# A decoder trunk whose first mixer loads and sums the conditioning weights at three rates instead of one

## The chip, the cores and the metric

The kernel runs on one core of one Trainium2 chip. Its time is the device time of one execution in microseconds (us). Each kernel is run several times and the median is compared.

## What is computed

Two layers of a decoder trunk for 256 tokens of width 2048. Layer 0 mixes with an S5 state space beside a gated delta rule, layer 1 with gated linear attention; each is followed by a SwiGLU feed-forward part. Every sub-layer is conditioned by a vector c: six vectors of 2048 values per layer (shift, scale and gate of the mixer, shift, scale and gate of the feed-forward part) come from one product with a large matrix.

```python
def ada_modulation(c, w, b):                 # w: 2048 x 12288
    mod = jax.nn.silu(c) @ w + b
    return jnp.split(mod[:, None, :], 6, axis=-1)
...
for i in range(DEPTH):
    sh_m, sc_m, gt_m, sh_f, sc_f, gt_f = ada_modulation(c, aw, ab)
    h = rmsnorm(x, m_pre) * (1.0 + sc_m) + sh_m
    x = x + gt_m * rmsnorm(mixer(h), m_post)
    h = rmsnorm(x, f_pre) * (1.0 + sc_f) + sh_f
    x = x + gt_f * rmsnorm(swiglu(h, wg, wu, wd), f_post)
```

The first mixer splits `h @ w_in0` into the S5 input, the q, k and v of the delta rule, a gate z and two small columns; the outputs of both head groups go through `w_out0`.

## The kernel before, in words

**Weights.** All weights are float32 and come in tiles of 128x1024 (512 KB) through one ring of six buffers, `w`, in the order of SyncE's queue (`wraw`, L228). A weight tile of a product is split into a rounded part on ScalarE (`wh`, L159) and a remainder on VectorE (`wl`, L160), with a ring of three buffers each, and TensorE multiplies three times (`mm3`, L234 to L236). A product works through its weights in pieces of two tiles, and after each piece it calls `tick(1)`.

**Streams.** A stream is a generator with a rate. A tick adds the rate to the stream's account, and each whole unit takes one step. So the rate is steps per piece of two weight tiles. The step's instructions are written there in program order, and a scheduler then orders each engine's instructions by their data and priorities. The streams of the first mixer are `chain` (the S5 recurrence, `s5_run`), `solve` (the delta rule's matrices, then its output) and `ada` (the conditioning).

**The conditioning (`ada`).** A section of 2048 values is done in two halves of 16 weight tiles each, one tile per step. There are three sections in the first mixer's list, so 96 steps. The first, the mixer's own gate `gm0`, is in the form for TensorE: the first of each four steps loads four tiles and sums them by 16 small matmuls (`row_sums`, L329). The other two, the shift and the scale `sf0` of the feed-forward part, are in the form for VectorE: each step loads one tile and adds it, times a value of silu(c), to an accumulator of 128x1024 (L355). At the end of a half 16 small matmuls (L365) sum the accumulator over the partitions. Each half begins with a memset and two small transfers on GpSimd (L340, L341, and L398 for a gate), which stand in a fixed order in its queue.

**The first mixer (`mixer0`)**, from about 165 us to 591 us of the span, has these stages, with their ticks:

- the convolved part of `w_in0` (q, k, v): eight products of two pieces, 16 ticks, behind a small product of an eighth of a tick. After the fourth (c = 6) the stream `solve` starts. The second four are the values v.
- the gate z: two products of four pieces, 8 ticks, while `solve` does the delta rule's matrices.
- the gate of the S5 part (`s5_glu`): 4 ticks.
- the first half of `w_out0` (`out_part`): 8 ticks, beside the end of `solve` (`gdn_out`).
- the second half of `w_out0` (`post`): 8 ticks. During its last two (n = 3) `ada` is held still (`quiet`). The residual x is loaded anew here on ScalarE's queue.

After that `post` forms the root of the mean square of one token block on VectorE (L134 to L139), adds the block to x (L527), and calls `pre`, which normalises x again, turns it by matmuls (L458) and applies the shift and scale that `need("sf0")` asks for. Steps of `ada` that are still missing then are taken at once.

Of the kernel before, what the change touches and what calls it, by code (L numbers as in the profile page):

```python
# [31 lines left out]
BOOST = (100, 100, 100)  # L32

PREP = 1.4
AR = (2.2, 1.25, 1.04, 0.3)
RS = (1.2, 2.0)
RG = (1.52, 1.8, 4)

# [5 lines left out]
class Net:  # L44
# [1463 lines left out]
    def mixer0(s, h, pu, G, then):  # L1508
        nc, a = s.nc, s.a
        W = a["w_in0"]  # L1510
        K16 = list(range(16))
        cw = s.small([P, 4, 16], tag="gd_cw", bufs=1)
        cr = s.small([P, 512], tag="t", bufs=6)[:64, :P]
        s.pin(nc.scalar.dma_start(out=cr, in_=a["gdn_conv_w"].rearrange("k (m p) -> (k m) p", p=P)))
        pc = s.tp()
        nc.tensor.transpose(pc[:, :64], cr, s.ident[:64, :64])
        nc.vector.tensor_copy(cw[:].rearrange("p k m -> p (k m)"), pc[:, :64])
        nw = s.small([P, P], tag="gd_nw", bufs=1)
        s.pin(nc.scalar.dma_start(out=nw, in_=a["gdn_norm_w"].partition_broadcast(P)))
        ya, parts, ybh, ybl = [], [], [], []  # L1520
        s.stream("chain", [s.s5_run(pu, ya)], RS[0])
        s.step("chain")
        pab = s.gemm_feat(W, 4096, K16, h, nw=16)
        beta, g, gc = s.gdn_gates(pab)
        dst = []
        for c in range(0, 16, 2):
            ps = s.gemm_feat(W, 1024 + c * P, K16, h)
            if c % 4 == 0:
                dst.append(s.b(name="qkv"))
            for i in range(2):  # L1530
                o = dst[-1][:, ((c + i) % 4) * 256 : ((c + i) % 4) * 256 + 256]
                s.gdn_conv(ps[i][:, :256], c + i, o, cw)
            if c == 6:
                s.stream("solve", [s.gdn_solve(dst, beta, g, gc, parts)], RG[0])
                s.streams["chain"][1] = RS[1]
        s.streams["solve"][1] = RG[1]
        zw = []
        for n in range(2):
            ps = s.gemm_tok(W, 3072 + n * 512, 512, K16, h)
            for t in range(NT):  # L1540
                if n == 0:
                    zw.append(s.b(name="zw"))
                zs = zw[t][:, n * 512 : n * 512 + 512]
                nc.scalar.activation(out=zs, in_=ps[t], func=AF.Silu)
                zv = zs.rearrange("p (h n) -> p h n", h=4)
                nc.gpsimd.tensor_tensor(out=zv, in0=zv, in1=nw[:].unsqueeze(1).to_broadcast([P, 4, P]), op=ALU.mult)
        s.finish("chain")
        s.streams["solve"][0].append(s.gdn_out(parts, zw, ybh, ybl))
        s.streams["solve"][1] = RG[2]
        s.boost = BOOST[2]  # L1550
        yah, yal = s.s5_glu([y[0] for y in ya], [y[1] for y in ya], [y[2] for y in ya])
        y = s.out_part(a["w_out0"], list(range(8)), s.chunks(yah, yal), None)
        s.finish("solve")
        x = s.load_x(nc.scalar, late=True)
        get = s.chunks(ybh, ybl)
        s.post(a["w_out0"], list(range(8, 16)), lambda k: get(k - 8), y, x, G(), lambda t: then(x, t), 8)
        return x


    def run(s, out):  # L1560
# [13 lines left out]
        def into(S, H):  # L1574

            tiles = []

            def then(x, t):
                if not tiles:
                    tiles.extend(s.h_tiles())  # L1580
                s.pre(x[t], t, s.need(S), s.need(H), *tiles)

            return then, lambda: s.chunks(*tiles)

        def store(x, t):
            for i in range(4):
                eng = nc.scalar if i % 2 else nc.sync
                eng.dma_start(out=out[0, t * P : t * P + P, i * 512 : i * 512 + 512], in_=x[t][i // 2][:, i % 2 * 512 : i % 2 * 512 + 512])
# [4 lines left out]
        s.boost = BOOST[1]  # L1593
        s.stream("ada", ada[:s.NA], AR[0])
        then, h1 = into("sf0", "hf0")
        x = s.mixer0(h, pu, lambda: s.need("gm0"), then)
        s.boost = 1
        s.streams["ada"][1] = AR[1]
        s.streams["ada"][0] += ada[s.NA :]
        then, h2 = into("sm1", "hm1")  # L1600
        s.ffn(h1(), 0, x, lambda: s.need("gf0"), lambda t: then(x, t))
        s.streams["ada"][1] = AR[2]
        then, h3 = into("sf1", "hf1")
        s.gla(h2(), x, lambda: s.need("gm1"), lambda t: then(x, t))
        s.streams["ada"][1] = AR[3]
        s.ffn(h3(), 1, x, lambda: s.need("gf1"), lambda t: store(x, t))
# [40 lines left out]
```

## Time and profile before

| what | us |
|---|---|
| median of 3 runs | 2556.36 (2548.6 to 2563.09) |
| the profiled execution, its own time | 2552.04 |
| its span, first to last instruction | 2550.3 |
| TensorE busy in the span | 2433.1 (95%) |
| VectorE busy | 1722.2 (68%) |
| mean granted TensorE clock | 0.978 of full speed |

TensorE is busy almost everywhere, but its busy time is modelled and says little by itself. So the mixer is read by stages: how long a stage lasts, how many matmuls it holds, which engine or transfer TensorE waits for in it, and what the transfers move.

### The profile page before, as it was taken

The page shows a single profiled execution, that of the slowest core. Times are in us where ns is not written, and L with a number is a line of the kernel's source. Part 1 is how long each engine was busy: PE and PEld are TensorE (multiplying, and loading weights), DVE is VectorE, ACT ScalarE, POOL GpSimd, SP SyncE. Part 2 cuts the span into 40 slices and gives each one's busy share as a digit, 9 for nine tenths or more (in the row PEclk, how much of TensorE's full clock was granted, in tenths as well). Part 3 has the DMA queues.
Part 4 walks back from the last instruction along what each step waited for, and adds up shares of the span by engine and source line. Part 5 has one row for each costly group of instructions (what it writes and reads, how often), then busy time and mean ns, then how long its engine had stood idle before and what let it go on. Part 6 is the DMA issues. An engine that isn't in the chain of part 4 may idle for free.

```text
span 2550.3 us, 43246 instructions
## 1 busy us (share of the span) xinstructions
PE 2433.1 (95%) x17510; PEld 2141.5 (84%) x17510; DVE 1722.2 (68%) x2268; ACT 1106.1 (43%) x1385; POOL 91.1 (4%) x153
## 2 busy tenths in 40 slices
PE   5999998997999999999998999999999999999998
PEld 2578877876899899989987897787799889988996
DVE  6856786878677766777778676677655544545456
ACT  3354552435344444433435533444544444443443
POOL 1120011000000000000000000000000000000000
PEclk8999998998999999999999999999999999999999
DMA  8877566686798888998886596788467666666664
GB/s 282 322 245 261 176 214 215 204 312 226 244 313 292 305 285 290 309 317 314 289 273 216 155 289 224 242 282 271 164 215 225 197 191 194 195 190 194 195 191 140
DMA packets 299017, 615.70 MB, mean 241 GB/s; under 512 B 24368, under 2 KB 61680, under 8 KB 298816
## 3 DMA queue, kind: packets, MB, share of 16 engines
q1 hardware_dynamic: 294240, 604.32, 71.5%
q0 software_dynamic: 2304, 4.93, 0.6%
q10 hardware_dynamic: 2272, 3.68, 0.4%
q8 instruction: 137, 2.24, 0.3%
q14 instruction: 64, 0.52, 0.1%
HBM read 610.10 MB, written 2.10 MB: 240 GB/s over the span
## 4 chain that ended last, share of the span: by engine, by line
PE 77%; DVE 8%; DMA 8%; ACT 3%; issue 3%; POOL 0%; ACTq 0%; DVEq 0%; SPq 0%
PE mm L236 23%; PE mm L235 23%; PE mm L234 23%; DMA w<-in_ada_w_dram 6%; DVE wl L160 2%; DVE small L355 1%; PE tp L329 1%; PE tp L365 1%; DMA w<-in_w_out_dram 1%; ACT small L462 1%; ACT small L421 1%; PE tp L1049 1%; ACT wh L159 0%; PE tp L400 0%; DMA w<-in_w_in_dram 0%
## 5 line engine op out<-in xcount | busy, mean ns | idle before, releaser
L159 ACT CAST wh<-w 128x1024 fp32r<-128x1024 f32 x722 | 758.0, 1051 | 1095.6 <-PE mm L235 550.6
L160 DVE TENSOR_TENSOR wl<-w,wh 128x1024 fp32r<-128x1024 f32 x722 | 874.1, 1220 | 476.0 <-ACT wh L159 474.9
L236 PE MATMUL mm<-hhi,wl 128*128 128x256 f32 (+1 forms) x3104 | 865.1, 279 | 10.0 <-DVE wl L160 10.0
L234 PE MATMUL mm<-hhi,wh 128*128 128x256 f32 (+1 forms) x3104 | 866.2, 279 | 0.0
L235 PE MATMUL mm<-hlo,wh 128*128 128x256 f32 (+1 forms) x3104 | 863.3, 278 | 0.0
L236 PEld LDWEIGHTS mm<-hhi,wl 128*128 128x128 f32 (+1 forms) x3104 | 582.8, 188 | 15.2 <-DVE wl L160 13.2
L235 PEld LDWEIGHTS mm<-hlo,wh 128*128 128x128 f32 (+1 forms) x3104 | 583.2, 188 | 2.0 <-issue 1.1
L234 PEld LDWEIGHTS mm<-hhi,wh 128*128 128x128 f32 (+1 forms) x3104 | 581.3, 187 | 4.1 <-issue 2.0
L355 DVE SCALAR_TENSOR_TENSOR small<-w,silu_c,small 128x1024 f32<-128x1024 f32 x288 | 369.0, 1281 | 195.8 <-DMA w<-in_ada_w_dram 187.3
L236 PE MATMUL mm<-wh,alo 128*128 128x512 f32 x656 | 258.2, 394 | 0.0
L235 PE MATMUL mm<-wl,ahi 128*128 128x512 f32 x656 | 256.9, 392 | 0.0
L234 PE MATMUL mm<-wh,ahi 128*128 128x512 f32 x656 | 256.2, 391 | 0.0
L234 PE MATMUL mm<-wh,hhi 128*128 128x512 f32 x440 | 177.1, 406 | 8.1 <-DVE hhi L467 4.2
L235 PE MATMUL mm<-wl,hhi 128*128 128x512 f32 x440 | 177.8, 404 | 3.5 <-DVE wl L160 2.2
L236 PE MATMUL mm<-wh,hlo 128*128 128x512 f32 x440 | 175.2, 399 | 0.7 <-DVE hlo L468 0.7
L235 PEld LDWEIGHTS mm<-wl,ahi 128*128 128x128 f32 x656 | 123.1, 188 | 29.1 <-issue 0.5
L234 PEld LDWEIGHTS mm<-wh,ahi 128*128 128x128 f32 x656 | 123.2, 188 | 27.2 <-ACT wh L159 0.5
L236 PEld LDWEIGHTS mm<-wh,alo 128*128 128x128 f32 x656 | 123.3, 188 | 25.1
L234 PEld LDWEIGHTS mm<-wh,hhi 128*128 128x128 f32 x440 | 83.8, 192 | 27.7 <-ACT wh L159 5.5
L236 PEld LDWEIGHTS mm<-wh,hlo 128*128 128x128 f32 x440 | 84.6, 192 | 22.3 <-issue 2.3
L235 PEld LDWEIGHTS mm<-wl,hhi 128*128 128x128 f32 x440 | 84.4, 192 | 22.4 <-DVE wl L160 3.9
L329 PE MATMUL tp<-w,silu_c 128*32 128x512 f32 x384 | 67.0, 645 | 11.6 <-DMA w<-in_ada_w_dram 6.7
(438 smaller groups left out, 2325.5 us busy)
## 6 DMA issues: line engine op xcount, KB each, us to landing
w<-in_ada_w_dram SPq DMA_DIRECT2D x384, 512.0 KB, 5.2
w<-in_ffn_gate_dram SPq DMA_DIRECT2D x176, 512.0 KB, 4.6
w<-in_ffn_up_dram SPq DMA_DIRECT2D x176, 512.0 KB, 4.5
w<-in_ffn_down_dram SPq DMA_DIRECT2D x176, 512.0 KB, 4.5
w<-in_w_in_dram SPq DMA_DIRECT2D x160, 512.0 KB, 5.2
w<-in_w_out_dram SPq DMA_DIRECT2D x64, 512.0 KB, 5.3
w<-in_s_glu_w_dram SPq DMA_DIRECT2D x8, 512.0 KB, 5.0
x<-in_x_dram SPq DMA_DIRECT2D x4, 512.0 KB, 6.4
```

The costliest lines, as they stand in the source:

```text
L159: s.nc.scalar.copy(hi, x)
L160: s.subs.append(s.nc.vector.tensor_tensor(out=lo, in0=x, in1=hi, op=ALU.subtract).ins)
L234: mm(ps, lhsT=lhs[0], rhs=rhs[0], start=st, stop=False)
L235: mm(ps, lhsT=lhs[0], rhs=rhs[1], start=False, stop=False)
L236: mm(ps, lhsT=lhs[1], rhs=rhs[0], start=False, stop=en)
L329: s.nc.tensor.matmul(ps[32 * j : 32 * j + 32, :], lhsT=lhsT, rhs=w, start=first, stop=last)
L355: nc.vector.scalar_tensor_tensor(out=acc, in0=wv[:, 0], scalar=s.sc[:, g : g + 1], in1=acc, op0=ALU.mult, op1=ALU.add)
L365: s.nc.tensor.matmul(ps[:, m : m + 1], lhsT=acc[:, m * P : m * P + P], rhs=e[:, 0:1], start=True, stop=True)
L421: s.nc.scalar.activation(out=dump[:, : int(x.free_size())], in_=x, func=AF.Square, accum_out=out)
L462: nc.scalar.activation(out=hf[:, js], in_=ps[:, js], func=AF.Identity, scale=S[:, k : k + 1], bias=H[:, k : k + 1])
L1049: nc.tensor.matmul(pp[:, i * 64 : i * 64 + 64], lhsT=s.s5_win[ig][e][:, i * P : i * P + P], rhs=us[:, i * 64 : i * 64 + 64], start=True, s ...
```

## The change

The rate of `ada` in the first mixer was 2.2 throughout. It is now 3.2 up to c = 6 (8 of the 16 ticks of q, k and v), 1.6 during the values, and 2.6 from the gate z on.

```diff
-AR = (2.2, 1.25, 1.04, 0.3)
+AR = (3.2, 1.25, 1.04, 0.3)
+AM = (1.6, 2.6)
...
             if c == 6:
                 s.stream("solve", [s.gdn_solve(dst, beta, g, gc, parts)], RG[0])
                 s.streams["chain"][1] = RS[1]
+                s.streams["ada"][1] = AM[0]
         s.streams["solve"][1] = RG[1]
+        s.streams["ada"][1] = AM[1]
```

The 96 steps and all other work are the same; only places change. In the code after the change the line numbers are higher by two (L230 is L228, L529 is L527). Three places follow.

SyncE's queue at the start of the mixer: `w<-in_ada_w_dram 128x1024` is a conditioning tile, `w<-in_w_in_dram` a tile of the mixer's own weights. Before:

```order
L228 DMA w<-in_w_in_dram 128x16x16
L228 DMA w<-in_w_in_dram 128x4x256 x2
L228 DMA w<-in_ada_w_dram 128x1024 x4
L228 DMA w<-in_w_in_dram 128x4x256 x4
L228 DMA w<-in_ada_w_dram 128x1024 x4
```

After:

```order
L230 DMA w<-in_w_in_dram 128x16x16
L230 DMA w<-in_w_in_dram 128x4x256 x2
L230 DMA w<-in_ada_w_dram 128x1024 x4
L230 DMA w<-in_w_in_dram 128x4x256 x2
L230 DMA w<-in_ada_w_dram 128x1024 x4
```

The second group of four conditioning tiles now stands two weight tiles earlier; so do later ones, until seven of the eight groups are in the first half of q, k and v.

SyncE's queue at the end of the mixer, before:

```order
L228 DMA w<-in_w_out_dram 128x2x512 x2
L228 DMA w<-in_ada_w_dram 128x1024 x2
L228 DMA w<-in_w_out_dram 128x2x512 x4
L228 DMA w<-in_ada_w_dram 128x1024 x4
L228 DMA w<-in_ffn_gate_dram 128x2x512 x8
```

After:

```order
L230 DMA w<-in_w_out_dram 128x2x512 x2
L230 DMA w<-in_ada_w_dram 128x1024 x3
L230 DMA w<-in_w_out_dram 128x2x512 x12
L230 DMA w<-in_ffn_gate_dram 128x2x512 x8
L230 DMA w<-in_ffn_up_dram 128x2x512 x2
```

The last twelve tiles of `w_out0` stand alone, and the four conditioning tiles behind them are gone.

VectorE at the end of the mixer, where the first token block's root (L134 to L139) leads to the addition to x (L527). L514 takes a finished product out of PSUM, L374 finishes a piece of the scale `sf0`. Before:

```order
L134 TENSOR_SCALAR small<-small 128x1
L355 SCALAR_TENSOR_TENSOR small<-w,silu_c,small 128x1024
L136 TENSOR_SCALAR small<-small 128x1
L514 TENSOR_TENSOR y<-mm,y 128x512
L138 TENSOR_SCALAR small<-small 128x1
L355 SCALAR_TENSOR_TENSOR small<-w,silu_c,small 128x1024
L139 SCALAR_TENSOR_TENSOR small<-small 128x1
L160 TENSOR_TENSOR wl<-w,wh 128x1024
L138 TENSOR_SCALAR small<-small 128x1
L374 SCALAR_TENSOR_TENSOR S_sf_102<-tp,vcols 128x4
```

After:

```order
L516 TENSOR_TENSOR y<-mm,y 128x512
L518 TENSOR_TENSOR y<-y,gate 128x512
L136 TENSOR_SCALAR small<-small 128x1
L138 TENSOR_SCALAR small<-small 128x1
L140 TENSOR_SCALAR small<-small 128x1
L141 SCALAR_TENSOR_TENSOR small<-small 128x1
L140 TENSOR_SCALAR small<-small 128x1
L141 SCALAR_TENSOR_TENSOR small<-small 128x1
```

The root's small instructions now stand next to each other; the conditioning's sums (L355 before), its L374 and two remainders (L160) between them have gone elsewhere.

## Rows read from the trace of the kernel before

**Rows 1.** The page, part 1: busy us, share of the span, instructions.
```profile
PE 2433.1 (95%) x17510; PEld 2141.5 (84%) x17510; DVE 1722.2 (68%) x2268; ACT 1106.1 (43%) x1385; POOL 91.1 (4%) x153
```

**Rows 2.** Windows by stage: length, busy us of engines, clock, DMA share, GB/s.
```profile
165.00:246.00 81.00, 76.89 (x688) 63.09 (x686) 47.56 (x76) 37.14 (x54) 8.64 (x17) 0.98 0.71 231
246.00:332.00 86.00, 81.14 (x800) 72.60 (x799) 66.05 (x117) 44.86 (x65) 3.62 (x9) 0.98 0.62 208
332.00:428.00 96.00, 83.42 (x1334) 70.26 (x1334) 75.03 (x100) 38.32 (x52) 16.51 (x21) 0.89 0.62 205
428.00:472.00 44.00, 44.00 (x619) 42.58 (x615) 30.65 (x41) 24.05 (x41) 0.00 (x0) 0.89 0.63 206
472.00:536.00 64.00, 56.83 (x274) 46.30 (x274) 55.32 (x111) 26.38 (x35) 1.50 (x2) 0.95 0.73 244
536.00:591.50 55.50, 50.00 (x210) 38.84 (x208) 43.30 (x51) 21.22 (x32) 1.43 (x2) 0.94 0.90 324
591.50:616.50 25.00, 12.60 (x61) 11.69 (x60) 19.83 (x52) 12.81 (x35) 1.99 (x3) 0.66 0.40 130
```

**Rows 3.** PE timeline, two neighbouring matmuls of the mixer's last product: start, us.
```profile
576.00 0.39 PE L235 MATMUL mm<-wl,ybhi 128*128 128x512 f32 x1
576.23 0.39 PE L236 MATMUL mm<-wh,yblo 128*128 128x512 f32 x1
```

**Rows 4.** What PE waited for in 536:591.5: us, times, longest.
```profile
PE mm L234 <- ACT wh L159: 3.9, 2, 3.5
```

**Rows 5.** DVE timeline at the mixer's end: start, us.
```profile
588.58 0.68 DVE L514 TENSOR_TENSOR y<-mm,y 128x512 f32<-128x512 f32 x1
...
590.98 0.20 DVE L134 TENSOR_SCALAR small<-small 128x1 f32<-128x1 f32 x1
591.10 1.27 DVE L355 SCALAR_TENSOR_TENSOR small<-w,silu_c,small 128x1024 f32<-128x1024 f32 x1
...
599.65 2.74 DVE L527 SCALAR_TENSOR_TENSOR x<-y,small,x 128x512 f32<-128x512 f32 x4
```

**Rows 6.** PE timeline at the mixer's end; in brackets the idle time before.
```profile
594.46 3.57 PE L365 MATMUL tp<-ones,small 128*128 128x1 f32 x16 [2.96 <-DVE small L355]
606.38 3.97 PE L458 MATMUL tp<-small,x 128*128 128x128 f32 x17 [8.35 <-issue]
```

**Rows 7.** DVE timeline at the end of the first feed-forward part.
```profile
1369.95 0.69 DVE L514 TENSOR_TENSOR y<-mm,y 128x512 f32<-128x512 f32 x1 [0.93 <-PE mm L236]
...
1374.04 2.08 DVE L527 SCALAR_TENSOR_TENSOR x<-y,small,x 128x512 f32<-128x512 f32 x3
```

**Rows 8.** Windows of line L329 alone (row sums): length, PE and PEld busy.
```profile
165.00:246.00 81.00, 12.84 (x80) 2.49 (x80) 0.98 0.71 231
246.00:332.00 86.00, 5.77 (x48) 1.25 (x48) 0.98 0.62 208
```

**Rows 9.** Windows of line L355 alone: length, DVE busy.
```profile
246.00:332.00 86.00, 3.83 (x3) 0.98 0.62 208
332.00:428.00 96.00, 25.55 (x20) 0.89 0.62 205
428.00:472.00 44.00, 11.53 (x9) 0.89 0.63 206
472.00:536.00 64.00, 20.49 (x16) 0.95 0.73 244
536.00:591.50 55.50, 18.30 (x15) 0.94 0.90 324
```

**Rows 10.** SyncE's queue, timeline: start, us, transfers issued.
```profile
198.50 2.84 SPq L228 DMA_DIRECT2D w<-in_ada_w_dram  x4
201.45 8.38 SPq L228 DMA_DIRECT2D w<-in_w_in_dram  x4
209.92 4.84 SPq L228 DMA_DIRECT2D w<-in_ada_w_dram  x4
```

**Rows 11.** The chain of waits, 140:640, at the third group.
```profile
200.99 7.30 DMA w<-in_ada_w_dram
208.34 1.92 PE tp L329 x8
```

**Rows 12.** What PE waited for in 472:536.
```profile
PE tp L537 <- DVE small L1428: 5.1, 3, 3.7
```

## The prediction
> **What bounds the kernel now.** I read four views: the page's busy times, the windows by stage, the waits of TensorE by stage, and VectorE's timeline at the mixer's end. The page says only that TensorE has little room [rows 1]; the change acts in the first mixer alone, so the stages decide [rows 2].
>
> The last product (536 to 591.5) is not bound by its matmuls. They follow each other at 0.23 us [rows 3], so its 8 ticks of 24 need 8 x 24 x 0.228 = 43.8 us; it lasts 55.5. Its transfers run at 0.90 busy and 324 GB/s [rows 2], and TensorE waits 3.9 us for a weight's rounded part [rows 4] that follows a transfer. At 324 GB/s a tile of 512 KB (0.524 MB) costs 1.62 us. Transfers set this stage.
>
> The 15 us behind it (591.5 to 606.4) are bound by VectorE. From taking the last product of the first token block out of PSUM (588.58) to the addition to x (599.65) are 11.1 us [rows 5]; the same path at the end of the first feed-forward part takes 1374.04 - 1369.95 = 4.1 [rows 7]. Between stand conditioning sums, one of which also holds TensorE for 2.96 us; TensorE then idles 8.35 us until L458 [rows 6].
>
> Earlier the picture is different. In q, k and v TensorE is busy 95% and 94% of the two halves, with transfers at 0.71 and 0.62 [rows 2]: there is room for transfers, none for matmuls. In the gate z VectorE is busy 78%, in the first half of `w_out0` 86% (55.3 of 64) [rows 2]: little room for sums there, and TensorE already waits 5.1 us for VectorE in the latter [rows 12].
>
> **The change part by part.** First the steps, which are rate times ticks:
>
> before: q, k 17.9; v 17.6; z 17.6; S5 gate 8.8; first `w_out0` half 17.6; second half 13.2 (six ticks, then held); rest 3.3. After: 26.0; 12.8; 20.8; 10.4; 20.8; 5.2; 0. Both sum to 96. The first 32 are the row sums on TensorE, four tiles at a time: 5 groups in the first half of q, k and v before, 7 after. The other 64 are sums on VectorE: 3.5, 17.6, 8.8, 17.6, 13.2, 3.3 from v on before; 6.8, 20.8, 10.4, 20.8, 5.2, 0 after. The trace shows 3, 20, 9, 16, 15 in these windows [rows 9], the same up to the queue's lag.
>
> *The mixer's end.* The four sums and the L374 that stood in the root's path go away; the order lists them gone. The path shrinks from 11.1 to the 4.1 of the clean place [rows 5, 7]: -7.0. It could be -8, because the L514 at 588.58 itself stood behind a sum; it could be -5, if something else is late next. What is late next is the rest of the path, the second root and L458, 6.7 us from L527 to L458 [rows 5, 6], which stays. I take -7.
>
> *The second half of `w_out0`.* It loses 8 tiles out of 13.2 in its ticks. Left are 16 weight tiles, 4 of x and 5.2 of conditioning, 25.2 x 1.62 = 41 us, now below the 43.8 of matmuls. At best it falls by 55.5 - 43.8 - 1.8 (one half's L365) = 9.9. But the x tiles and the conditioning's last five come at its start, where 3.5 of the 3.9 us wait was one wait [rows 4], and that stays. I take -6.5 (-3 to -9.9).
>
> *The first half of `w_out0`.* Plus 3.2 tiles and 3.2 sums at 18.30 / 15 = 1.22 us on VectorE [rows 9]: 3.9 us if nothing hides them. VectorE has 8.7 us free of 64 there [rows 2], and transfers 4.6 tiles per tick, 7.4 us at 324 GB/s, 8 x 7.4 = 60 of 64. Some of it will show, because single ticks are shorter than the mean: +3 (0 to +5).
>
> A rule speaks against this piece. The Trainium skill, "DMA: Bandwidth & Descriptors", section Specifications, gives a limit of about 358 GB/s from HBM per core. The stage's 324 [rows 2] agree with it as a ceiling; as an estimate by that page, a tick of matmuls here (5.5 us) covers 1.97 MB, 3.7 tiles; both 2 + 2.2 and 2 + 2.6 are over, and the second costs 0.6 us more per tick, 4.7 over 8, where my own term is 3.
>
> *The gate z and the S5 gate.* Plus 3.2 and 1.6 sums, 5.9 us of VectorE. It has 21 us free in z and 13 in the S5 gate [rows 2], but the delta rule's chain runs through it, one short instruction at a time, and a sum ahead of a link delays the link: +1.5 (0 to +6).
>
> *q, k and v.* Two groups of row sums move from the second half to the first: at 16 matmuls each, 12.84 / 80 x 16 = 2.6 us or 5.77 / 48 x 16 = 1.9 [rows 8]. TensorE pays them in either half, so the move is neutral by itself. The second half gets 3.3 more sums, 4 us on an engine with 20 us free [rows 2]: 0. What can cost is the ring. Four of its six buffers hold a group until its row sums are done, and groups now come in almost every tick. In the trace a group is issued at 198.50 and its row sums start at 208.34, 9.8 us later [rows 10, 11], and last 1.9; that is 11.7 between groups if strictly one after the other, against 81 / 8 = 10.1 us per tick. Six groups stand one tick behind another: 6 x 1.6 = 9.6 at worst on this count. But much of the 7.30 us landing [rows 11] was shared with the weight tiles of the same tick, and up to three split tiles lie ahead. The first half has the room on average: 81 us x 231 GB/s = 18.7 MB, plus 8 tiles is 22.9 MB, 71 us at 324. I take +2.5 (-2 to +9.6), nearer to the hidden end. Below nothing, because TensorE may also use a group as filler where it idles now.
>
> On GpSimd the memset of the next half waits for the end of the last one, and a copy of the S5 chain stands behind it; both move earlier together. The chain has to end only before the S5 gate: 0. In the feed-forward parts the stream starts with another fraction, and its steps shift by a tick: 0 (-2 to +2).
>
> **Sum:** -7 - 6.5 + 3 + 1.5 + 2.5 = -6.5. Against the profiled execution's own 2552.04 this is 2545.5. That run lies 4.3 below the median of the runs shown, 2556.36; on the median the forecast is 2549.9, rounded to 2550.
>
> **The rivals.** *All of the gain, none of the cost.* The front hides everything and the last product becomes bound by matmuls: -9.9 - 8 = -18, 2538. For it: transfers at 0.62 to 0.73 up to 536 [rows 2]. Against: VectorE's 86% in the first half of `w_out0`, and TensorE's wait for it there [rows 12].
>
> *Paid back on VectorE.* The sums put into z, the S5 gate and the first half of `w_out0` all lie on the path, +6 and +5, and the ring costs +6: 17 against 13.5, +3.5, 2560. For it: the same 64 sums are merely elsewhere. Against: VectorE has free time in each stage.
>
> *Slower: the ring of six runs empty.* If a group and the two weight tiles behind it must wait for the group before, a tick's load is six tiles, 9.7 us, plus a landing of about 5, 14.9 us against 10.1 per tick; 4.8 x 6 = 29, and with the rest -9 the sum is +20, 2576. It decides (over 0.5%) from 22 us in q and k, 3.6 per group. For it: the group at 198.50 was waited for [rows 11]. Against: there the queue held four weight tiles per group and still ran at 0.71.
>
> That the change doesn't do what it says is excluded: the order shows the moved tiles.
>
> **How the numbers follow.** Forecast 0.50 (2544 to 2557), all of the gain 0.25 (about 2538), paid back 0.14 (about 2560), ring empty 0.11 (about 2576). The range that holds 8 in 10 leaves out half of the ring case and the outer tails: 2537 to 2566. About 0.5%, 12.8 us, is what a measurement of this kernel can tell from no change: faster means below 2543.6, slower above 2569.1. Faster gets the full-gain case and a little of the forecast's tail, 0.27; slower the ring case, 0.10; the same, 0.63.
>
> **What would show it.** In the trace after: from L514 of the first block to L527 (L529 there) about 4 us; TensorE's idle time before the L458 row shorter, and no wait of L365 there; the last product 47 to 50 us long with fewer than 7 sums in it; the first half of `w_out0` 65 to 69 us; q and k 81 to 87 us with 7 groups (112 row-sum matmuls), and waits of L329 for its tiles under 4 us in all. The prediction is wrong if q and k grow by more than 10 us (ring), if the last product stays above 53 us (then not the conditioning's tiles but x or the rounding bound it), or if the first half of `w_out0` grows by more than 6.

## The result, and the profile after

The changed kernel takes 2574.1 us (median; 2571.3 to 2580.0) where the kernel before takes 2558.1 in the same rounds: a ratio of 1.0065, 95% interval 1.0043 to 1.0087. It is slower by some 16 us. That lies above the range of the prediction (2537 to 2566), whose forecast of 2550 was a gain of 6.5 us.

The profiled executions stand the same way, spans of 2550.3 and 2569.6 us, so the traces hold the loss and it can be read stage by stage. Line numbers of after are 2 higher than those of before (L355 is L357). The page first, part 1, in answer to [rows 1]:

```profile
PE 2439.3 (95%) x17510; PEld 2143.4 (83%) x17510; DVE 1726.7 (67%) x2268; ACT 1108.5 (43%) x1388; POOL 93.7 (4%) x153
```

The same instructions, and 6 of the 19 us appear as TensorE's busy time. Then the windows by stage, cut where the stages begin in this trace, with the two cuts around v kept as before (q and k; v; gate z; S5 gate; first half of `w_out0`; second half; the mixer's end), in answer to [rows 2]: length, busy us of the engines, clock, DMA share, GB/s.

```profile
165.00:246.00 81.00, 78.27 (x681) 62.01 (x680) 45.41 (x71) 31.38 (x46) 9.30 (x18) 0.98 0.74 248
246.00:332.00 86.00, 81.76 (x794) 74.16 (x794) 67.85 (x123) 48.13 (x68) 3.11 (x7) 0.98 0.55 184
332.00:432.50 100.50, 87.98 (x1349) 73.25 (x1348) 83.03 (x108) 43.99 (x60) 18.10 (x21) 0.86 0.71 236
432.50:477.40 44.90, 42.60 (x625) 41.37 (x626) 28.15 (x34) 24.27 (x42) 2.38 (x3) 0.96 0.54 173
477.40:560.10 82.70, 60.45 (x274) 48.35 (x273) 63.58 (x124) 25.35 (x34) 1.45 (x2) 0.83 0.65 228
560.10:614.70 54.60, 50.38 (x209) 39.80 (x208) 39.64 (x54) 23.01 (x34) 1.44 (x2) 0.94 0.79 283
614.70:632.00 17.30, 10.11 (x47) 8.92 (x48) 14.62 (x43) 13.37 (x37) 0.56 (x1) 0.80 0.10 32
```

The first half of `w_out0` took 64 us before and takes 82.7. Set side by side by the first matmul of each stage (us from the span's start):

| stage begins | before | after | gained (-) or lost in the stage ahead |
|---|---|---|---|
| S5 gate | 428.2 | 432.4 | +4.2 (q, k, v up to their last tick 0.4; from there 3.8) |
| first half of `w_out0` | 472.1 | 477.4 | +1.1 |
| second half | 536.1 | 560.1 | **+18.7** |
| its last product ends | 591.5 | 614.7 | -0.8 |
| first feed-forward layer | 612.4 | 626.2 | **-9.4** |
| second mixer (L458) | 1381.2 | 1399.5 | +4.5 |
| end of the span | 2550.3 | 2569.6 | +1.0 |

Each figure of a stage comes from one execution. Some versions of the experiments below run the same program up to a certain place and so repeat the stages ahead of it. frac is the changed kernel up to the feed-forward layer, post34 the kernel before up to the second half. The windows of the half, and TensorE's wait in it, in frac and then in post34:

```profile
480.80:564.60 83.80, 61.17 (x275) 48.55 (x274) 63.10 (x123) 25.43 (x34) 1.45 (x2) 0.84 0.64 224
PE tp L539 <- DVE small L1430: 18.9, 4, 11.2
...
472.90:537.30 64.40, 57.04 (x275) 46.36 (x274) 54.97 (x112) 26.51 (x35) 1.50 (x2) 0.95 0.72 243
PE tp L539 <- DVE small L1430: 5.3, 3, 3.7
```

So the loss in the half repeats: 82.7 and 83.8 us against 64.0 and 64.4. The stages ahead of it repeat less well. From the first matmul of q, k and v to the start of their last tick the pair (the traces of before and after) has 157.3 and 157.5 us. With it, the five traces with 2.2 there (post34, late26, front22 and behind_before too) have 152.1 to 160.4, and the seven with 3.2 and 1.6 (frac, hold, narrow_after, place_after, back22 and behind_after too) have 157.4 to 161.4. The means, 156.0 and 159.1, differ by 3.2 us where the pair shows almost nothing. From there to the half the pair has 149.8 and 154.8 us, but the means of three traces each (post34 and late26 with before, frac and hold with after) are 152.6 and 153.6. Ahead of the half some 4 to 7 us are lost; how they divide between these stages the pair doesn't show.

What TensorE waited for in the first half of `w_out0`, in answer to [rows 12] (us in total, times, longest), and its timeline at the two long waits (start, us; the idle time before stands in brackets):

```profile
PE tp L539 <- DVE small L1430: 18.7, 4, 11.0
...
PE mm L236 <- ACT wh L161: 1.7, 1, 1.7
```

```profile
485.37 0.40 PE L238 MATMUL mm<-wh,yalo 128*128 128x512 f32 x1
496.77 1.16 PE L539 MATMUL tp<-ident,small 128*128 128x128 f32 x4 [11.01 <-DVE small L1430]
505.15 0.66 PE L539 MATMUL tp<-ident,small 128*128 128x128 f32 x2 [7.22 <-DVE small L1430]
```

L539 transposes the delta rule's normed output, L1430 writes it. This output comes in four pieces (two groups of heads by two token blocks), each behind a reduction (L1419), an inverse root in some fourteen short instructions, and four products (L1430). I call these the four roots. VectorE's timeline in the first of them:

```profile
478.71 0.67 DVE L1419 TENSOR_REDUCE small<-small 128x4 f32<-128x512 f32 x1
...
481.42 1.28 DVE L357 SCALAR_TENSOR_TENSOR small<-w,silu_c,small 128x1024 f32<-128x1024 f32 x1
482.61 0.15 DVE L1424 TENSOR_TENSOR small<-small 128x4 f32<-128x4 f32 x1
482.73 1.29 DVE L357 SCALAR_TENSOR_TENSOR small<-w,silu_c,small 128x1024 f32<-128x1024 f32 x1
483.93 0.16 DVE L148 TENSOR_SCALAR small<-small 128x4 f32<-128x4 f32 x1
...
496.28 1.13 DVE L1430 SCALAR_TENSOR_TENSOR small<-tp,small,zw 128x128 f32<-128x128 f32 x4
```

Conditioning sums of 1.28 us stand between the 0.15 us steps of the root: seven sums (9.0 us) and four weight splits (L162, 4.9 us) in all. The root takes 17.6 us from L1419 to L1430, and TensorE has nothing to do for 11.0 of them.

The kernel before interleaves sums as well, but in its third root, 17.4 us long with eight sums. There TensorE waits 3.70 us (behind it, the root's first step and its products on VectorE):

```profile
504.84 0.40 PE L236 MATMUL mm<-wh,yalo 128*128 128x512 f32 x1
508.94 1.16 PE L537 MATMUL tp<-ident,small 128*128 128x128 f32 x4 [3.70 <-DVE small L1428]
...
491.05 0.69 DVE L1417 TENSOR_REDUCE small<-small 128x4 f32<-128x512 f32 x1 [1.08 <-ACT small L1413]
508.44 1.12 DVE L1428 SCALAR_TENSOR_TENSOR small<-tp,small,zw 128x128 f32<-128x128 f32 x4
```

Its first two roots hold no sum and take 4.5 and 7.6 us. The difference is what TensorE has in hand: between the input of the third root and its transposes stand 58 matmuls of `w_out0` (13 us at 0.23). After the change 36 stand ahead of the first root's transposes (8 us, part of them gone when the root begins), and none between the first root's transposes and the second's.

The change moved the sums from one root to the other by arriving further on. At the end of each half of a conditioning (every 16 steps) the stream stops until VectorE's last sum, TensorE (L365), GpSimd's memset and the bias have gone by. Before, the stream stands at step 64 during the first two roots, which keeps sums out of them. After, it is 6 steps further on when the first root begins, and stops at step 80, behind the second root.

At the mixer's end the gain came as priced. VectorE's path, in answer to [rows 5, 7], and TensorE's next start, in answer to [rows 6]:

```profile
609.27 0.69 DVE L516 TENSOR_TENSOR y<-mm,y 128x512 f32<-128x512 f32 x1 [2.32 <-PE mm L238]
...
613.36 2.74 DVE L529 SCALAR_TENSOR_TENSOR x<-y,small,x 128x512 f32<-128x512 f32 x4
```

```profile
620.09 5.25 PE L460 MATMUL tp<-small,x 128*128 128x128 f32 x23 [5.42 <-issue]
```

4.1 us from L516 to L529, and no sum between.

### The profile page after: what moved, and what is told of

The parts are those of the page before. It is cut to its first block, busy times and chain, and to the rows that moved or that the text cites. A ratio compares the mean times of both kernels' runs of the same rounds, so it can differ in the third digit from the quotient of the medians.

```text
span 2569.6 us, 43234 instructions
## 1 busy us (share of the span) xinstructions
PE 2439.3 (95%) x17510; PEld 2143.4 (83%) x17510; DVE 1726.7 (67%) x2268; ACT 1108.5 (43%) x1388; POOL 93.7 (4%) x153
## 4 chain that ended last, share of the span: by engine, by line
PE 71%; DVE 11%; DMA 10%; issue 3%; ACT 3%; POOL 0%; DVEq 0%; ACTq 0%; POOLq 0%; SPq 0%
PE mm L238 21%; PE mm L237 21%; PE mm L236 21%; DMA w<-in_ada_w_dram 8%; DVE wl L162 3%; DVE small L357 2%; PE tp L331 2%; DMA w<-in_w_out_dram 1%; ACT wh L161 1%; PE tp L367 1%; ACT small L464 1%; ACT small L423 1%; PE tp L1051 1%; DMA w<-in_ffn_down_dram 1%; PE tp L402 1%
## 5 line engine op out<-in xcount | busy, mean ns | idle before, releaser
L162 DVE TENSOR_TENSOR wl<-w,wh 128x1024 fp32r<-128x1024 f32 x722 | 875.5, 1221 | 486.0 <-ACT wh L161 478.7
L357 DVE SCALAR_TENSOR_TENSOR small<-w,silu_c,small 128x1024 f32<-128x1024 f32 x288 | 371.1, 1289 | 195.2 <-DMA w<-in_ada_w_dram 190.6
L236 PEld LDWEIGHTS mm<-wh,hhi 128*128 128x128 f32 x440 | 83.8, 192 | 25.7 <-ACT wh L161 3.7
L331 PE MATMUL tp<-w,silu_c 128*32 128x512 f32 x384 | 70.7, 650 | 9.8 <-ACT silu_c L325 5.1
```

The lines of the kernel that those rows point to most:

```text
L162: s.subs.append(s.nc.vector.tensor_tensor(out=lo, in0=x, in1=hi, op=ALU.subtract).ins)
L236: mm(ps, lhsT=lhs[0], rhs=rhs[0], start=st, stop=False)
L331: s.nc.tensor.matmul(ps[32 * j : 32 * j + 32, :], lhsT=lhsT, rhs=w, start=first, stop=last)
L357: nc.vector.scalar_tensor_tensor(out=acc, in0=wv[:, 0], scalar=s.sc[:, g : g + 1], in1=acc, op0=ALU.mult, op1=ALU.add)
```

## The experiments

The theory at first, which I call 'place': sums inside the first two roots keep TensorE waiting. Its rivals: 'amount' or 'rate' (2.6 sums a step are too much for VectorE wherever they stand), 'front' (the rates ahead of the gate z), and later 'ring and queue' (a conditioning tile whose sum is late holds one of the six buffers, and SyncE's in-order queue keeps the next weight tiles back).

**Sums queued behind the root.** In both kernels, the conditioning comes last in a tick and its sums are ordered behind the latest root.

```
+        for name in sorted(s.streams, key=lambda n: s.gout and n == "ada"):
...
+                    with s.tc.issue_after(s.root) if s.root is not None else nullcontext():
                         nc.vector.scalar_tensor_tensor(out=acc, in0=wv[:, 0], ...)
```

> The changed kernel with its rates kept (3.2, 1.6, 2.6), but while the delta rule's output runs, the conditioning takes its step last in a tick, and its sums on VectorE are queued behind the last instruction of the latest root of the delta rule's norm. The order has no sum in any of the four roots (7 and 3 in the first two of the changed kernel). Theory 'place' (the changed kernel loses because sums stand between the small instructions of the first two roots, and TensorE stops at the turn behind them): TensorE's wait for VectorE at that turn falls from 18.7 us to under 5, and the time to 3 to 10 us below the kernel before. Rival 'amount' (2.6 sums per tick are too many for VectorE in the gate z and the first half of w_out0, wherever they stand): still 8 to 16 us above the kernel before. Rival 'front' (3.2 in q and k costs): likewise 10 to 16 us above.

> The kernel before with 2.2 throughout and the same queueing behind the roots (0, 0, 8, 4 sums in the four roots before, none now). Theory 'place': the smaller wait there (5.1 us) goes, 2 to 6 us below the kernel before. Rivals 'amount' and 'front': no change, within 2 us.

Measured: 2572.8 (ratio 1.0050, 1.0028 to 1.0072) and 2568.9 (1.0038, 1.0018 to 1.0059). All four roots are clean in both (3.6 to 6.7 us long in behind_after), yet the half takes 84.3 and 80.0 us. What TensorE, then ScalarE, waited for there in the first of them:

```profile
PE mm L238 <- ACT wh L163: 9.1, 3, 7.8
PE mm L239 <- DVE wl L164: 7.6, 4, 5.1
PE tp L542 <- DVE small L1433: 3.2, 4, 1.4
```

```profile
ACT wh L163 <- DMA w<-in_w_out_dram: 47.3, 12, 8.1
```

The wait at the transposes is gone (3.2) and another has taken its place: rounded weights, which wait for their transfer, while transfers are busy 0.66 of the stage. Sums that are held keep their tiles in the ring, and the `w_out0` tiles stand behind them in SyncE's queue, which waits 31.2 us for sums (L360) in this half, where it waits 11.8 for them (L357) in the changed kernel. So 'place' as I had put it (order the sums behind the root, and the time comes back) fell: a sum held back costs as much as one let in.

**The two parts of the change alone.** front22 has 2.2 up to the gate z and 2.6 from there; back22 has 3.2 and 1.6, then 2.2.

```
-AR = (3.2, ...); AM = (1.6, 2.6)
+AR = (2.2, ...); AM = (2.2, 2.6)      front22
+AR = (3.2, ...); AM = (1.6, 2.2)      back22
```

> 2.2 through q, k and v as in the kernel before, 2.6 from the gate z on. The order has 8 and 3 sums in the first two roots. Theory 'place': as slow as the changed kernel, 13 to 18 us above the kernel before. Rival 'amount': the same, 13 to 18 above. Rival 'front': within 4 us of the kernel before.

> 3.2 in q and k and 1.6 in v as in the changed kernel, 2.2 from the gate z on as before. The order has 0, 7, 0, 3 sums in the four roots. Theory 'place': one root of the first pair is held by 7 sums (about 9 us), so part of the loss stays: 3 to 10 us above the kernel before. Rival 'amount': the loss is gone, 5 below to 2 above. Rival 'front': the loss stays whole, 13 to 18 above.

Measured: 2567.7 (1.0043, 1.0021 to 1.0065) and 2567.8 (1.0036, 1.0017 to 1.0054). The half takes 78.5 and 72.2 us, with 8, 3, 0, 1 and 0, 7, 0, 3 sums in the four roots, and TensorE waits 17.7 and 13.5 at the transposes. back22 has the old rate there and still loses 8 us, and its second root is the one that holds sums. Each part alone costs more than half of what both cost. 'Front' allowed front22 4 us over the kernel before; it is some 11 over, with the front of the kernel before. 'Amount' had the loss gone in back22; it is 9 to 11 over. 'Place' had named 13 to 18 for front22, so it missed the total too, though the half is as slow as it says.

**Conditioning out of the half.** Rate 0 in the first half of `w_out0`; in early the steps go to the front instead.

```
+        s.streams["ada"][1] = 0.0
         y = s.out_part(a["w_out0"], list(range(8)), ...)
         s.finish("solve")
+        s.streams["ada"][1] = 2.8      (early: 1.2, with 2.2 and 3.4 ahead)
```

> The changed kernel, with the conditioning stopped during the eight steps of the first half of w_out0 (rate 0 there) and at 2.8 a step in the second half, which had none left to do in the changed kernel. The stretch from the first product of the first half to the first of the second took 82.7 us in the changed kernel, 64.0 before. Theory 'conditioning among the norm's roots' (the sums of the conditioning, the four roots and the weight tiles of w_out0 share VectorE, the ring of six and SyncE's queue there): the stretch falls to 54 to 60 us, as long as the second half without conditioning (54.5); the second half keeps 54 to 56, since its 2.2 a step cost it nothing before (55.4); the tail at the mixer's end comes back by 3 to 8 us; 2574 - 25 + 5 = 2554, 2548 to 2560. Theory 'norm alone' (the roots and their chain of results on TensorE take their time there whatever the conditioning does, and the kernel before was lucky in the placing of the roots): the stretch stays above 70 us and the total above 2562.

> As the one before it, but the steps taken out of the first half of w_out0 go to the front: 3.2 up to the values, 2.2 during the matrices, 3.4 in the gate z and the S5 gate, 0 in the first half of w_out0, 1.2 after it. Theory 'conditioning among the norm's roots': the first half of w_out0 takes 54 to 60 us. If the front absorbs the steps as it did q, k and v at 3.2 (cost 0.5 us in the changed kernel) it costs under 5 us, and the total is 2545 to 2555; if the ring of six runs empty at 3.4 tiles a step the gate z and the S5 gate grow by 10 us or more over the 132.2 us that they took in the changed kernel (345.2 to 477.4), and the total is 2560 to 2575.

Measured: 2561.7 (1.0026, 1.0013 to 1.0039) and 2566.0 (1.0048, 1.0034 to 1.0062). The windows of the two halves of hold:

```profile
482.00:542.90 60.90, 53.99 (x258) 43.73 (x258) 43.12 (x105) 26.64 (x35) 0.00 (x0) 0.97 0.52 173
542.90:600.60 57.70, 50.27 (x209) 39.54 (x207) 46.04 (x53) 19.78 (x30) 1.45 (x2) 0.94 0.88 315
```

Without conditioning the half takes 60.9 us, 22 less (54 to 60 were expected): the conditioning is the cause, not the roots alone. The rest of the gain goes at the mixer's end, which is long again (26.7 us from the last product to the feed-forward layer, 11.5 in the changed kernel), since the last sums now fall there. In early the half takes 65.0, but it begins at 493.5, 16 us later than in the changed kernel: 3.4 tiles a step do not go by the gate z and the S5 gate unnoticed.

**Ring and queue.** own gives the conditioning tiles two of the six buffers and GpSimd's queue; ring5 is the kernel before with five buffers.

```
-                    wv = s.wraw(Wv[:, g : g + 1, c0 : c0 + 1024], 1, 1024)
+                    wa = s.ring.tile([P, 1024], F32, tag="wa", name="wa", bufs=2)
+                    s.pin(nc.gpsimd.dma_start(out=wa, in_=Wv[:, g, c0 : c0 + 1024]))
...
-    WB = 6
+    WB = 4      (ring5: 5, and the tiles as before)
```

> The changed kernel, with the weight tiles of the conditioning in a ring of their own of two buffers, loaded from GpSimd's queue; the other weight tiles keep four of the six buffers and SyncE's queue to themselves. Same steps, same sums, same order of them. Theory 'ring and queue' (a conditioning tile whose sum waits behind a root holds one of the six buffers, SyncE's in-order queue stops at the next tile, and the w_out0 tiles behind it come late): the first half of w_out0 takes 56 to 68 us where the changed kernel took 82.7, and no wait of SyncE's queue there is above 10 us (20.8 in the changed kernel). Theory 'amount' (2.6 sums a step and the roots are more than VectorE can do in that stretch, whoever loads the tiles): it stays at 80 us or more. With four buffers the rest of the kernel may be slower by some us in either case, so the stretch decides, not the total.

> The kernel before with a ring of five buffers for weight tiles in place of six, nothing else. Theory 'ring and queue': the stretches with the most tiles a step lose most; the first half of w_out0, 64.0 us with six, takes 72 us or more with five, and the total is 2565 to 2600. Theory 'amount': VectorE does the same work, five buffers are enough for tiles that land in about 5 us, the stretch takes 62 to 66 us and the total is 2553 to 2562.

Measured: own 2721.9 (1.0657, 1.0623 to 1.0691), the half 76.2 us; ring5 2592.9 (1.0150, 1.0119 to 1.0181), the half 62.2 us:

```profile
487.10:549.30 62.20, 54.82 (x275) 44.26 (x274) 53.41 (x112) 25.36 (x34) 1.50 (x2) 1.00 0.68 229
```

ring5 tells most. A buffer less costs 35 us, but not here: the half begins 15 us later than before, the second half is 4.6 us longer, and the first feed-forward layer takes 784.9 us in place of 768.8. With the sums in the last two roots again (0, 0, 6, 6), five buffers are enough in this half. own settles little: its half lies between the two expectations, and SyncE's queue still waits up to 29.4 us. But with a queue for the conditioning alone, TensorE's wait at the transposes remains:

```profile
PE tp L542 <- DVE small L1433: 15.5, 4, 8.3
```

**The sums' time taken away.** narrow_after is the changed kernel with the 32 sums of the last conditioning 64 columns wide in place of 1024. They then take 0.28 us each, their tiles are loaded as before, and most of that work is left out.

```
+                    nn = 64 if (layer, sec) == (0, 4) else 1024
+                    nc.vector.scalar_tensor_tensor(out=acc[:, :nn], in0=wv[:, 0, :nn], ...)
```

> The changed kernel, with the 32 sums of the last of the three conditionings (the scale of the first feed-forward layer) only 64 columns wide in place of 1024, so that they take a small part of their time; their weight tiles are loaded all the same. It leaves out that part of the work. Theory 'VectorE's time' (the time of the sums among the roots is what TensorE waits for): the first half of w_out0 takes 58 to 66 us in place of 82.7, although the tiles come through the same ring and queue, and the total is 2545 to 2558. Theory 'transfers' (the loading of 2.6 tiles a step beside the w_out0 tiles is what is late): it stays above 74 us.

Measured: 2548.7 (0.9961, 0.9936 to 0.9986). The window of the half, and TensorE's wait:

```profile
477.90:538.40 60.50, 54.90 (x274) 44.16 (x273) 41.33 (x120) 25.27 (x34) 1.44 (x2) 1.00 0.83 291
```

```profile
PE tp L540 <- DVE small L1431: 3.1, 3, 1.8
```

The same tiles through the same ring and queue, 2.6 a step: 60.5 us, with the transfers busier (0.83) than in any other version of this half. It is the sums' 1.28 us on VectorE, not their loading. Short sums also give their buffers back sooner. So this version alone doesn't tell how much the time of the sums costs in the roots and how much through tiles that are held; TensorE's wait at the transposes, 3.1 in place of 18.7 us, speaks for the roots.

**Two rates by two places.** late26 is the kernel before with 2.6 from the first half of `w_out0` on, which leaves its first two roots without sums; place_after is the changed kernel with 2.0 in the gate z and the S5 gate, which moves the sums to the last two roots; early22 is the kernel before with 2.8 in place of 2.2 during the values alone (the expectation calls these eight ticks those of the delta rule's matrices), which moves them to the first two.

```
before       2.2 up to the values, 2.2 values,   2.2 z and S5 gate, 2.2 first half of w_out0
late26       2.2                   2.2           2.2                2.6
early22      2.2                   2.8           2.2                2.2
after        3.2                   1.6           2.6                2.6
place_after  3.2                   1.6           2.0                2.6
```

> The kernel before, with 2.6 steps in place of 2.2 from the first half of w_out0 on, so the same rate there as in the changed kernel; nothing else. With these rates the end of a half of the conditioning (step 64) falls between the norm's second and third root, as in the kernel before: by the order of the instructions no sum stands in the first two roots, 9 and 6 in the last two (changed kernel: 7 and 3 in the first two). Theory 'place' (what a sum costs there depends on whether it stands in a root that TensorE meets early in the half): the first half of w_out0 takes 62 to 68 us, TensorE's wait for the roots at its transposes (L537) stays under 8 us, and the mixer's end gets shorter, since the conditioning ends 2 steps earlier: total 2548 to 2560. Theory 'rate' (2.6 sums a step are too many for VectorE or for the ring, wherever they stand): 75 us or more there and a total above 2565.

> The kernel before, 2.2 steps a weight tile as it has them, but 2.8 during the eight tiles of the delta rule's matrices, so that the conditioning arrives at the first half of w_out0 some 5 steps further on. There the rate is 2.2 again, and only the place differs: by the order of the instructions 7 and 2 sums stand in the first two roots, 0 and 0 in the last two (kernel before: 0, 0, 8, 4). Theory 'place': the first half of w_out0 takes 72 to 84 us in place of 64.0, TensorE's wait for the roots at its transposes is 12 us or more in place of 5.1, and the total is 2562 to 2576. Theory 'rate' (2.6 in that stretch is the cause, 2.2 fits): 62 to 68 us, a wait under 8 us, total 2553 to 2562.

> The changed kernel, with 2.0 steps in place of 2.6 in the gate z and the S5 gate alone; 3.2, 1.6 and, from the first half of w_out0 on, 2.6 stay. By the order the first two roots then hold no sum, the last two 10 and 4 (changed kernel: 7, 3, 0, 0). Theory 'place': the first half of w_out0 takes 64 to 72 us in place of 82.7, TensorE's wait at its transposes is under 8 us in place of 18.7, and the total is 2553 to 2565. Theory 'rate': 75 us or more, total 2568 or more. The conditioning ends later than in the changed kernel, so up to 9.5 us of what this gives back can go at the mixer's end.

Measured: late26 2561.9 (1.0003, 0.9983 to 1.0023), early22 2567.0 (1.0050, 1.0026 to 1.0074), place_after 2563.6 (1.0030, 1.0014 to 1.0047). TensorE's wait at the transposes and the window of the half, in this order:

```profile
PE tp L539 <- DVE small L1430: 5.7, 3, 4.2
...
473.00:541.50 68.50, 60.68 (x291) 49.67 (x290) 54.26 (x113) 26.69 (x35) 2.93 (x4) 0.93 0.71 246
```

```profile
PE tp L539 <- DVE small L1430: 14.3, 4, 7.7
...
483.10:554.60 71.50, 56.20 (x274) 45.96 (x273) 54.14 (x117) 26.82 (x35) 1.45 (x2) 0.90 0.69 221
```

```profile
PE tp L539 <- DVE small L1430: 8.7, 2, 8.1
...
483.40:553.00 69.60, 58.97 (x291) 48.28 (x290) 56.20 (x116) 26.40 (x35) 2.93 (x4) 0.90 0.74 242
```

| first half of `w_out0`, us (wait at the transposes) | most sums in the last two roots | most sums in the first two |
|---|---|---|
| 2.2 a step | 64.0 (5.1) before | 71.5 (14.3) early22; 72.2 (13.5) back22 |
| 2.6 a step | 68.5 (5.7) late26; 69.6 (8.7) place_after | 82.7 (18.7) after; 78.5 (17.7) front22 |

The place costs 7.5 to 8.2 us at the old rate and 9 to 14 at the new one; the rate costs 4.5 to 5.6 in the good place. Part of this is that in late26 and place_after a second end of a conditioning half falls into this stage: 32 matmuls of L367 (3.7 us busy) in place of 16 (1.8). Some figures miss 'place' by a little: the half of late26 (68.5, up to 68 expected, in the slowest of its ten executions), its total (up to 2560), the half of early22 (71.5, from 72) and the wait in place_after (8.7, under 8). All lie nearer to 'place' than to 'rate', which had 75 us or more for late26 and place_after, and 62 to 68 for early22. early22 loses 0.5% of the whole kernel by a shift of 5 steps, at no higher rate in this half. Not all of that is the half: in early22, back22 and place_after it also begins 11 to 13 us later than before (483.1, 485.1, 483.4; before 472.1), or 8 to 11 us counted from the first matmul of q, k and v. Against the means above, 1 to 5 us of this arise in q, k and v, and 4 to 5 in the gate z and the S5 gate; part comes back at the mixer's end. That difference isn't explained by the roots and stays open; the table compares the half alone.

**The account, and the part that worked.** frac is the changed kernel entering the feed-forward layer with the fraction that the kernel before has there; post34 is the kernel before with 3.4 in the second half of `w_out0`.

```
+        s.streams["ada"][2] = 0.675          frac, at the feed-forward layer
+        s.streams["ada"][1] = 3.4            post34, ahead of the second half (and the line above)
```

> The changed kernel, with one line more: the conditioning's account of steps is set to 0.675 where the first feed-forward layer begins. The kernel before enters with 0.675 there, the changed one with 0, and by this alone the conditioning's steps fall on other weight tiles in the feed-forward layer. Theory 'phase': the 4.6 us that the changed kernel lost between the mixer's end and the second mixer (894.6 to 899.4, from the first product of the feed-forward layer in us) come back, total 2568 to 2571. Theory 'carried over' (what is late comes from the mixer's end): they stay, and the total is 2572 to 2576.

> The kernel before, with 3.4 steps in place of 2.2 in the second half of w_out0 alone, and the account set to 0.675 where the feed-forward layer begins, as the kernel before has it there. Up to the second half nothing is changed. It takes the one part of the change that worked (the conditioning is done before the mixer's last norm, which then runs without sums: 9.5 us less from the mixer's last product to the feed-forward layer's turn) without the part that cost (the sums in the first two roots). Theory: the second half of w_out0 takes the same 55 us within 2 us, since 2.2 steps a tile there cost nothing beside none; the end falls from 20.9 us (last product of w_out0 to the first of the feed-forward layer) to 11 to 13; total 2546 to 2550. If 3.4 tiles a step beside its weights are too many for the transfers there, the half grows by 5 to 10 us, and the total is within 3 us of the kernel before or above it.

Measured: frac 2569.3 (1.0036, 1.0011 to 1.0062), post34 2560.0 (1.0001, 0.9980 to 1.0021). The stretch that frac was about has two wrong figures in its expectation (894.6 and 899.4); the traces have 768.8 us before and 773.3 after, from the layer's first product to L458. In frac it is 773.8: the 4.5 us did not come back, and by this 'phase' fell. The total, 2569.3, would fit 'phase' (2568 to 2571), but its interval overlaps that of the changed kernel, so it decides nothing. Over the other kernels of this study, ring5 and own left out, the stretch runs from 764.8 to 773.8 without any order by fraction. post34 enters the layer with the fraction of the kernel before, runs the same program from there, and has 772.9 us. So 4.5 us is hardly more than single executions of the same work differ by in this stretch.

In post34 the mixer's end shrinks as expected (11.8 us where the kernel before has 20.9), but the second half takes it back. Its window, and TensorE's wait there:

```profile
537.30:606.10 68.80, 55.13 (x225) 43.06 (x223) 50.33 (x64) 22.08 (x32) 2.87 (x4) 0.88 0.87 300
```

```profile
PE mm L236 <- ACT wh L161: 11.5, 3, 6.5
```

68.8 us in place of 55.4, a loss above the 5 to 10 us that the expectation named for too many transfers. No version here beats the kernel before while doing all of its work.

## Why the prediction was wrong

**The mixer's end, -7: right, a little low.** L516 to L529 takes the 4.1 us forecast; -9.4 from the last product to the feed-forward layer (-9.9 in frac), where the bound was -8.

**The first half of `w_out0`, +3 (0 to +5): the step that failed, +18.7.** It priced 3.2 more sums at 1.22 us against VectorE's free time in the stage's mean (8.7 of 64 us, [rows 2]). As the price of the rate alone that was nearly right: 4.5 to 5.6 us where the place is good. Of the 25.8 us between the forecast sum (-6.5) and the traces (+19.3), 15.7 lie in this step. What it missed is that all sums of the stage are moved on by 6 steps, out of the third root into the first. The row that should have warned was at hand: [rows 12] has three waits of TensorE for the roots with the longest at 3.7 us, and a root with eight sums in it would cost far more where fewer matmuls stand ahead of its transposes. Of the 18.7 us by which the stage grew, 13.6 are this wait (18.7 after, 5.1 before); TensorE's busy time grew by 3.6 (60.45 less the 56.83 of [rows 2]) for the same 274 matmuls, at a granted clock of 0.83 in place of 0.95; 1.5 are left.

By the limit of some 358 GB/s in the Trainium skill ("DMA: Bandwidth & Descriptors", Specifications) the prediction estimated 4.7 us for this stage. The rate's 4.5 to 5.6 us look like it, but the stage ran at 246 GB/s with transfers busy 0.71 in late26, and at 291 without loss in narrow_after: the limit did not decide here. Nor is it a ceiling in these traces: the changed kernel moved 364 GB/s over 10.7 us (the windows of the last section).

**The second half, -6.5 (-3 to -9.9): too much, -0.8** (-3.3 in frac, with 52.1 us). The step said that transfers set this stage, by their 0.90 share. TensorE was busy 50.0 of its 55.5 us in the same row [rows 2], so no more than 5.5 could come back at that clock. The floor of 43.8 us took the 0.23 us spacing for all matmuls, where the granted clock of the stage is 0.94 and 18 others run. After, with transfers down to 0.79, TensorE is busy 50.4 of 54.6. The wait for a rounded weight, which was to stay, fell from 3.9 to 0.5 us, and one of 2.2 us for a sum (L357) came in its place. The sign of being wrong that the prediction set here, a last product above 53 us, came, with this busy TensorE in place of the late x tiles or rounding that it had supposed. The half's conditioning at 2.2 was hidden behind TensorE; at 3.4 (post34) it is not.

**Gate z and S5 gate, +1.5 (0 to +6): 4.9** in the pair, 1.0 by the means above. **q, k and v, +2.5 (-2 to +9.6): 0.4** in the pair, 3.2 by the means. Both are inside their bounds either way. The eighth tick begins 6.3 us later than before (243.0, 236.7), with the two groups more that were named, and in the pair v gives all of it back: its last tick begins at 322.6, before at 322.2. Windows of L331 alone (length, TensorE and weight loads busy), in answer to [rows 8]; the first window ends ahead of the seventh group, whose last row sum starts at 251.4, still ahead of v's first tick (252.6):

```profile
165.00:246.00 81.00, 16.24 (x96) 3.59 (x96) 0.98 0.74 248
246.00:332.00 86.00, 5.15 (x32) 1.07 (x32) 0.98 0.55 184
```

**Feed-forward parts, 0 (-2 to +2): 5.5**, of which 4.5 in the stretch where post34 alone differs by 4.1 from the kernel before.

**The rivals.** The slower one put the ring of six in q and k at 29 us. From their first matmul to v's first tick all eight traces with 3.2 there have 86.7 to 88.8 us, the six with 2.2 have 75.9 to 83.8 (ring5 and own left out): some 7 more in the mean, and v returns a part. The mechanism exists, as behind_after shows with its 47.3 us of late `w_out0` tiles and ring5 with its 35 us, but it is not where the change lost most. 'Paid back on VectorE' named the engine and the stage, and limited the price to the duration of the sums that were added (+5). But all sums of the stage changed place, and the chain that TensorE waits for now runs through ten of them while TensorE has little in hand. The prediction's own sign of failure for this stage, the half growing by more than 6 us, is what came.

## What to carry to other kernels

Price work that is moved onto an engine by what it is put between, not by the engine's free share: a 1.28 us sum between 0.15 us links of a chain adds its length to the chain each time, and costs nothing only while the engine that waits has work in hand. A change of rate is also a change of phase; look in the order for where every later piece lands, above all around the points at which the stream stops by itself. And an engine that is busy 90% in a stage bounds what taking away transfers can give there, whatever the transfers' own share.

## What the runs showed of the hardware

TensorE's granted clock paid for the wait a second time. Windows in the changed kernel: its last 8.6 us of matmuls, the long wait, the two transposes with the second wait between, the work behind them, and 10 us once the clock is back.

```profile
477.40:486.00 8.60, 8.36 (x38) 6.53 (x36) 7.78 (x12) 2.10 (x2) 0.00 (x0) 1.00 0.83 282
486.00:496.70 10.70, 0.00 (x0) 0.00 (x0) 9.29 (x19) 2.59 (x3) 0.00 (x0) 0.63 0.98 364
496.70:505.10 8.40, 1.16 (x4) 0.73 (x4) 8.02 (x25) 0.59 (x1) 0.00 (x0) 0.50 0.83 283
505.10:512.50 7.40, 6.67 (x27) 5.75 (x28) 2.73 (x7) 2.35 (x5) 0.00 (x0) 0.50 0.12 50
...
516.00:526.00 10.00, 9.73 (x44) 7.58 (x43) 8.73 (x31) 5.25 (x8) 0.00 (x0) 1.00 0.22 66
```

The clock is at 1.00 (2.4 GHz) up to the wait, falls in it, and is at 0.50 (1.2 GHz) for the 7.4 us of work that follow; half of the 6.67 us busy there, 3.3 us, is the lower level. The whole stage has 0.95 before [rows 2] and 0.83 after. The same rows show a second surprise: transfers, busy 0.98 during the wait, fall to 0.12 behind it. There SyncE's queue takes 20.82 us, from 501.28 on, to issue three conditioning tiles, 19.0 of them in one wait:

```profile
501.28 20.82 SPq L230 DMA_DIRECT2D w<-in_ada_w_dram  x3
```
